# A decoder layer on one core: the first two blocks of the mixer's output projection computed as a pair, with three units of seven products

## The chip, the cores and the metric

The kernel runs on one core of a Trainium2 chip, as one program and one launch. The time is the device time of that core in microseconds (us). Its engines are named as in the profile: PE is TensorE (PEld its weight loads), DVE is VectorE, ACT is ScalarE, POOL is GpSimd, and SP is the engine whose queue issues most of the loads. Every engine works through its own queue of instructions in order and waits on semaphores for the others.

## The reference, cut to what matters

One layer on 256 tokens of width 2048 in float32: a mixer of two attention branches, whose outputs are gated, added and projected by `w_out`, and then a gated feed-forward part (FFN). Each of the two has a norm ahead of it and one behind it.

```python
merged = g[:, :, 0] * (o_a @ w_o_mla) + g[:, :, 1] * (o_b @ w_o_swa)
y = merged @ w_out                          # (256 x 2048) @ (2048 x 2048)
x = x + rms_norm(y, norm_mix_post)
x = x + rms_norm(conv_ffn(rms_norm(x, norm_ffn_pre)), norm_ffn_post)
```

## The kernel before

**Products.** The 256 tokens are two tiles of 128. Every float32 operand is split into a high and a low part, and one product of 128 tokens x 128 rows of the weight x 512 columns is three matmuls (`mm3`: high x high, high x low, low x high). `gemm` takes a block of 512 columns in eight chunks of two weight rows of tiles: a chunk of 128x1024 values is loaded into a `raw` tile by SP's queue (`wchunk`), ACT copies its high part (`whi`, L143), DVE subtracts to get the low part (`wlo`, L144), and PE does 12 matmuls with it, six for each token tile.

**The ring.** `raw` tiles come from a ring of 3, pairs of `whi` and `wlo` from a ring of 4 (`RING`). Two more tiles, `flex`, belong to the one or the other: while `flex[0]` is `"raw"` there are five raw tiles and four pairs, while it is `"w"` there are three raw tiles and five pairs. A pair comes free when the last matmul that reads it has run. `extra` gives some chunks a pair of their own from another pool; `px` holds three (`EXTRA`).

**Pairs of blocks.** `pair_gemm` computes two blocks of 512 columns at once, in units of two weight rows of tiles. A plain unit is eight products. A unit of seven (`seven`) forms sums of weight quarters on DVE and of the tokens' quarters ahead of time (`token_sums`), does seven products and leaves their recombination to a few DVE additions at the end; its raw rows are loaded by POOL's queue. Before the change it is used in a gate projection (`cg` in the profile) and in the FFN.

**The order of work.** Stages stand one after the other in the program. `at(t, f)` places small work into a later step (`tick`) of a running projection. What comes out is put in order by a scheduler, which also moves independent instructions among each other, on every engine.

**The stage in question.** The merge with `wo_a` (four blocks; `m_cols` transposes the merged values) is followed by `w_out` in four blocks, all by `gemm`, and by the FFN's first block. Ahead of `w_out`, `flex[0]` is set to `"w"`. In the last block, `split=0` runs the eight chunks for token tile 0 alone, and the products of tile 1 (`todo`, `finish_tile`) follow, with all eight pairs still held: five of the ring and three of `px`. `y_evac` squares a finished block on ACT and multiplies it by the norm's gain (`gpost`) on DVE. As soon as tile 0 of the last block is finished, `resid(0)` forms the inverse root (`rsqrt`, some ten DVE instructions on 128x1), adds to the residual stream `x2` (L987), transposes it on PE (`x2T`, L990), and splits it into the FFN's operand on ACT (L994) and DVE (L997). `resid(1)` does the same for tile 1.

Of the kernel before, what the change touches and what calls it, by code (L numbers as in the profile page):

```python
# [23 lines left out]
KT = D // P  # L24
# [17 lines left out]
def trunk_layer(ctx, tc, x, x_cols_in, conv_cols_in, g_mix_post, g_ffn_post, w_in, w_q, w_kv,  # L42
                sinks, rel, wo_a, wo_b, w_out, w_up, w_down, rope_tab, strip_sel, out):
    nc = tc.nc
    vec, act, pe, pool = nc.vector, nc.scalar, nc.tensor, nc.gpsimd

    def open_pool(name, bufs=1, **kw):
        es = ExitStack()
        return es, es.enter_context(tc.tile_pool(name=name, bufs=bufs, **kw))
# [3 lines left out]
    pss = ctx.enter_context(tc.tile_pool(name="pss", bufs=2, space=PS))  # L53
# [5 lines left out]
    def sb(pl, shape, name, dt=F32, tag=None, bufs=None):  # L59
        return pl.tile(shape, dt, name=name, tag=tag or name, **({"bufs": bufs} if bufs else {}))  # L60
# [43 lines left out]
    flex = ["raw"]  # L104
    turn = dict(raw=0, w=0)
# [10 lines left out]
    def wchunk(src, shape, own=None, rawp=None, rbufs=1, parts=None):  # L116
        i = cnt[0]
        cnt[0] += 1
        n = int(np.prod(shape))
        raw = rawp.tile([P, 1024], F32, name=f"raw{i}", tag="xraw", bufs=rbufs) if rawp else \  # L120
            ring_tile("raw", f"raw{i}", F32, in_turn("raw"))
        dst = raw[:, :n]
        if len(shape) == 2:
            dst = dst.rearrange("p (a b) -> p a b", a=shape[0])
        elif len(shape) == 3:
            dst = dst.rearrange("p (a b c) -> p a b c", a=shape[0], b=shape[1])
        if len(shape) == 3:
# [27 lines left out]
    now = [0]  # L155

    def at(t, *fs):
        steps[max(t, now[0])].extend(fs)
# [6 lines left out]
    def drain():  # L165
        while steps:
            tick()

    def new_acc(tag, ps=None):
        i = cnt[0]  # L170
        pl, pt = ps or (pacc, "acc")
        return [pl.tile([P, 512], F32, name=f"acc{tag}_{i}_{t}", tag=pt) for t in range(NT)]

    def mm3(o, ah, al, bh, bl, start, stop):
        pe.matmul(o, ah, bh, start=start, stop=False)  # L175
        pe.matmul(o, ah, bl, start=False, stop=False)  # L176
        pe.matmul(o, al, bh, start=False, stop=stop)  # L177
# [486 lines left out]
    acc, _ = gemm(XH, XL, w_in, 0, KT, 0, 512)  # L664
# [4 lines left out]
    acc, _ = gemm(XH, XL, w_in, 0, KT, C_KV, KVR + ROPE)  # L669
# [78 lines left out]
    AH, AL = pair_view(ath), pair_view(atl)  # L748
# [138 lines left out]
    b = now[0] + 26  # L887
# [11 lines left out]
    for j in range(4):  # L899
        acc, _ = gemm(XH, XL, w_in, 0, KT, C_GA + 512 * j, 512)  # L900
# [10 lines left out]
    mt = [slot("a", p) for p in range(8)]  # L911
    mth, mtl = highs(mt), lows(mt)
    MH_, ML_ = pair_view(mth), pair_view(mtl)
    x2_all = [sb(p3, [P, D], f"x2_{t}") for t in range(NT)]
    x2 = [[x_[:, j * 512:(j + 1) * 512] for j in range(4)] for x_ in x2_all]
    es6, p6 = open_pool("p6")
    gpost = sb(p6, [P, D], "gpost", tag="gp")

    def late_loads(i):

        if i < 4:
            nc.sync.dma_start(gpost[:, i * 512:(i + 1) * 512], g_mix_post[i * 512:(i + 1) * 512].partition_broadcast(P))
        else:
            t, j = divmod(i - 4, 4)
            nc.sync.dma_start(x2[t][j], x[t * P:(t + 1) * P, j * 512:(j + 1) * 512])

    esx, px = open_pool("px", bufs=EXTRA)
    es4, p4 = open_pool("p4")

    def m_cols(p, ld):  # L930
        pt = pst.tile([P, 512], F32, name=f"mT{p}", tag="t")
        for i in range(2):
            for t in range(NT):
                c = (2 * (p % 2) + i) * P
                pe.transpose(pt[:, i * 256 + t * P:i * 256 + (t + 1) * P], ld[t][0][:, c:c + P], ident)
        split_to(mth[p][:, :], mtl[p][:, :], pt, 0.5)
# [8 lines left out]
            ld.append((a, b))  # L945
        return ld

    for i in range(12):
        at(now[0] + 10 + 2 * i, lambda i=i: late_loads(i))
    for j in range(4):  # L950
        ld = merge_loads(j)
        acc, _ = gemm(AH, AL, wo_a, 0, KT, 512 * j, 512)
        for t in range(NT):
            a, b = ld[t]
            vec.scalar_tensor_tensor(a, a, 1.0, acc[t], op0=ALU.add, op1=ALU.mult)
            vec.tensor_tensor(a, a, b, op=ALU.add)
        for p in range(2):
            at(now[0] + (3 if j == 3 else 1) + p, lambda p=2 * j + p, ld=ld: m_cols(p, ld))


    yg_all = [[sb(p6, [P, 1024], f"yg_{t}_{j}", tag="f" + "ab"[t], bufs=2) for j in range(2)] for t in range(NT)]
    yg = [[yg_all[t][j // 2][:, (j % 2) * 512:(j % 2 + 1) * 512] for j in range(4)] for t in range(NT)]
    blocks = [(0, 512), (512, 512), (1024, 512), (1536, 256), (1792, 256)]
    NB = len(blocks)
    W_BLOCKS = [(512 * j, 512) for j in range(4)]
    ssy = [sb(p3, [P, 4], f"ssy{t}") for t in range(NT)]
    jk = lambda name: sb(p6, [P, 512], name, tag="jk", bufs=1)

    def y_evac(acc, b, t):
        c0, n = W_BLOCKS[b]  # L970
        j, o = c0 // 512, c0 % 512
        act.activation(jk(f"yj{b}_{t}")[:, :n], acc[t][:, :n], AF.Square, accum_out=ssy[t][:, b:b + 1])
        vec.tensor_tensor(yg[t][j][:, o:o + n], acc[t][:, :n], gpost[:, c0:c0 + n], op=ALU.mult)

    x2hl = [slot("b", p) for p in range(8)]
    HH, HL = pair_view(highs(x2hl)), pair_view(lows(x2hl))
# [31 lines left out]
        vec.tensor_scalar(r2, r, 0.5, None, op0=ALU.mult)  # L1008
        rf[t] = (r, r2)

    flex[0] = "w"
    turn.update(raw=0, w=0)
    for b in range(4):
        c0, n = W_BLOCKS[b]
        last = b == 3
        acc, todo = gemm(MH_, ML_, w_out, 0, KT, c0, n, split=0 if last else None, extra={i: (px,) for i in range(EXTRA)} if last else None)
        if b == 0:
            drain()
            es4.close()
            es8, p8 = open_pool("p8")  # L1020
        if last:
# [264 lines left out]
    def pair_end(i):  # L1286
# [46 lines left out]
EXTRA = 3  # L1333
# [69 lines left out]
```

## Time and profile before

| what | us |
|---|---|
| time, median of 3 runs | 1468.56 (1468.35 to 1468.61) |
| the profiled execution's own time | 1470.05 |
| its span, first to last instruction | 1468.3 |
| PE busy in the span | 1456.9 |
| DVE busy | 1067.2 |
| ACT busy | 830.5 |
| POOL busy | 64.9 |

The profile is of one execution. A row of its timeline gives the start, the length, the engine, the line of the kernel, and the tiles written and read, in brackets the idle time ahead and what ended it. A window's row gives the busy time of each engine (with instructions in brackets), the granted clock of TensorE and the load of the DMA queues. Matmuls overlap: one of 512 columns shows some 0.39 us, though the next starts earlier. The wait view names two waits of PE for another engine, both in the first 5 us.

### The profile page before, as it was taken

How to read it: one execution, taken by the hardware profiler on the slowest of the kernel's cores; microseconds unless marked ns; L12 is line 12 of the kernel's file. 1: busy time of each engine (PE TensorE's matmuls, PEld its weight loads, DVE VectorE, ACT ScalarE, POOL GpSimd, SP SyncE). 2: the span in 40 equal slices, each digit the busy share in tenths (PEclk: the TensorE clock that was granted, in tenths of full speed). 3: DMA queues.
4: the chain of work that ended last, by engine and by line, in shares of the span. 5: the costliest groups of instructions: out<-in, count | busy, mean ns of one | idle time of the engine just before them, and what ended most of it. 6: DMA issues, size and time to landing. Idle time of an engine off the chain costs nothing.

```text
span 1468.3 us, 20938 instructions
## 1 busy us (share of the span) xinstructions
PE 1456.9 (99%) x7576; PEld 1244.8 (85%) x7576; DVE 1067.2 (73%) x1881; ACT 830.5 (57%) x1372; POOL 64.9 (4%) x113
## 2 busy tenths in 40 slices
PE   9999999999999999999999999999999999999997
PEld 7888888888888888888888888888888888888886
DVE  7688896745667665555699976778776687677775
ACT  7588874543555554444566655555454565555453
POOL 0011110000000000000000000000000000000000
PEclk9999999999999999999999999999999999999999
DMA  8755376466655559756766666665656666667573
GB/s 297 211 164 167 108 259 192 162 212 200 191 156 160 164 163 334 226 184 212 225 205 185 188 193 193 187 187 187 218 174 213 198 187 189 187 197 233 163 237 129
DMA packets 149909, 287.60 MB, mean 196 GB/s; under 512 B 18428, under 2 KB 29597, under 8 KB 149677
## 3 DMA queue, kind: packets, MB, share of 16 engines
q1 hardware_dynamic: 141312, 256.80, 56.5%
q0 software_dynamic: 8400, 29.41, 6.4%
q8 instruction: 59, 0.97, 0.3%
q14 instruction: 46, 0.37, 0.1%
q10 hardware_dynamic: 92, 0.05, 0.0%
HBM read 277.79 MB, written 8.44 MB: 195 GB/s over the span
## 4 chain that ended last, share of the span: by engine, by line
PE 97%; DVE 2%; ACT 1%; issue 0%; DMA 0%; DVEq 0%; ACTq 0%
PE accg L175 13%; PE accg L177 13%; PE accg L176 13%; PE ub L1147 10%; PE ua L1147 10%; PE ua L1151 5%; PE ub L1151 5%; PE cd L177 2%; PE cd L175 2%; PE cd L176 2%; PE cdb L175 1%; PE cdb L177 1%; PE cdb L176 1%; PE mpo L875 1%; PE cg L176 1%; PE cg L177 1%
## 5 line engine op out<-in xcount | busy, mean ns | idle before, releaser
L144 DVE TENSOR_TENSOR wlo<-raw,whi 128x1024 fp32r<-128x1024 f32 (+2 forms) x476 | 576.3, 1214 | 282.5 <-ACT whi L143 275.2
L143 ACT CAST whi<-raw 128x1024 fp32r<-128x1024 f32 (+2 forms) x476 | 494.7, 1043 | 427.5 <-PE accg L177 172.3
L175 PE MATMUL accg<-whi,ahl 128*128 128x512 f32 (+1 forms) x480 | 187.9, 392 | 0.0
L177 PE MATMUL accg<-whi,ahl 128*128 128x512 f32 (+1 forms) x480 | 185.6, 387 | 0.0
L176 PE MATMUL accg<-wlo,ahl 128*128 128x512 f32 (+1 forms) x480 | 184.8, 385 | 0.0
L1147 PE MATMUL ua<-ahl,whi 128*128 128x512 f32 x640 | 154.6, 391 | 0.0
L1147 PE MATMUL ub<-ahl,whi 128*128 128x512 f32 x640 | 154.6, 391 | 0.0
L175 PE MATMUL accg<-whi,bhl 128*128 128x512 f32 x378 | 148.2, 392 | 0.0
L177 PE MATMUL accg<-whi,bhl 128*128 128x512 f32 x378 | 147.4, 390 | 0.0
L176 PE MATMUL accg<-wlo,bhl 128*128 128x512 f32 x378 | 147.3, 390 | 0.0
L1147 PEld LDWEIGHTS ub<-ahl,whi 128*128 128x128 f32 x640 | 117.5, 188 | 22.9 <-ACT cc L1045 0.2
L1147 PEld LDWEIGHTS ua<-ahl,whi 128*128 128x128 f32 x640 | 117.6, 188 | 22.7
L177 PEld LDWEIGHTS accg<-whi,ahl 128*128 128x128 f32 x480 | 90.1, 188 | 18.0
L176 PEld LDWEIGHTS accg<-wlo,ahl 128*128 128x128 f32 x480 | 90.3, 188 | 15.6
L175 PEld LDWEIGHTS accg<-whi,ahl 128*128 128x128 f32 x480 | 90.3, 188 | 15.5
L1151 PEld LDWEIGHTS ub<-ahl,wlo 128*128 128x128 f32 x640 | 82.2, 191 | 3.2
L1151 PEld LDWEIGHTS ua<-ahl,wlo 128*128 128x128 f32 x640 | 82.2, 191 | 3.1
L1151 PE MATMUL ua<-ahl,wlo 128*128 128x256 f32 x640 | 83.7, 283 | 0.0
L177 PEld LDWEIGHTS accg<-whi,bhl 128*128 128x128 f32 x378 | 71.0, 188 | 14.8
L176 PEld LDWEIGHTS accg<-wlo,bhl 128*128 128x128 f32 x378 | 71.0, 188 | 14.5
L1151 PE MATMUL ub<-ahl,wlo 128*128 128x256 f32 x640 | 83.2, 283 | 0.0
L175 PEld LDWEIGHTS accg<-whi,bhl 128*128 128x128 f32 x378 | 71.0, 188 | 14.3
(545 smaller groups left out, 2218.9 us busy)
## 6 DMA issues: line engine op xcount, KB each, us to landing
raw<-in_ffn_w_up_dram SPq DMA_DIRECT2D x176, 512.0 KB, 4.5
raw<-in_w_in_dram SPq DMA_DIRECT2D x105, 512.0 KB, 4.5
raw<-in_ffn_w_down_dram SPq DMA_DIRECT2D x68, 512.0 KB, 4.5
raw<-in_w_o_swa_dram SPq DMA_DIRECT2D x32, 512.0 KB, 4.4
raw<-in_w_o_mla_dram SPq DMA_DIRECT2D x32, 512.0 KB, 4.5
raw<-in_w_out_dram SPq DMA_DIRECT2D x32, 512.0 KB, 4.1
bias<-strip POOLq DMA_DIRECT2D x16, 256.0 KB, 4.4
raw<-in_mla_w_q_up_dram SPq DMA_DIRECT2D x32, 128.0 KB, 2.8
```

The lines of the kernel that those rows point to most:

```text
L143: act.copy(hi[:, a:b], raw[:, a:b])
L144: vec.tensor_tensor(lo[:, a:b], raw[:, a:b], hi[:, a:b].bitcast(F32), op=ALU.subtract)
L175: pe.matmul(o, ah, bh, start=start, stop=False)
L176: pe.matmul(o, ah, bl, start=False, stop=False)
L177: pe.matmul(o, al, bh, start=False, stop=stop)
L875: pe.matmul(o, w(t), p_[:, c], start=n == 0, stop=n == 5)
L1147: pe.matmul(acc[i], hi[:, c], hn[p][:, j * 512:(j + 1) * 512], start=p + j == 0, stop=stop)
L1151: pe.matmul(acc[i][:, 0:256], lo[:, c], hn[p][:, j * 512:j * 512 + 256], start=False, stop=False)
```

## The change

Blocks 0 and 1 of `w_out` become one `pair_gemm` of eight units in the order `ppspspsp` (p plain, s seven). The sums of the tokens' quarters for its three sevens (`m_sums`) are formed during the last two blocks of `wo_a`, in tiles of `px`. The raw rows of the first and third seven lie in `px` too, those of the second in the tile that `gpost` takes afterwards; so `gpost` is loaded later, by POOL's queue. The sums of the weight quarters take the place of `yg_all[t][1]`. `pair_evac` adds the recombined part, squares it and multiplies by the gain. Blocks 2 and 3 stay with `gemm`. The accumulators of the last `wo_a` block and of block 2 move to other PSUM banks. `flex[0] = "w"` now stands behind the `w_out` loop.

```diff
-    gpost = sb(p6, [P, D], "gpost", tag="gp")
+    gpost = []
...
-            nc.sync.dma_start(gpost[:, i * 512:(i + 1) * 512], g_mix_post[i * 512:(i + 1) * 512].partition_broadcast(P))
+            if i == 0:
+                gpost.append(sb(p6, [P, D], "gpost", tag="gp"))
+            pool.dma_start(gpost[0][:, i * 512:(i + 1) * 512], g_mix_post[i * 512:(i + 1) * 512].partition_broadcast(P))
...
+    def m_sums(u):
+        st = sb(px, [P, 1024], f"ms{u}", F32R, tag="w" + ("hi", "lo")[u % 2])
+        ms[u] = token_sums(mt[u].bitcast(F32), yg[0][0], yg[0][1], st[:, 0:512], st[:, 512:1024])
...
+        if j == 2:
+            for u in range(W_ORDER.count("s")):
+                at(now[0] + 2 + 4 * u, lambda u=u: m_sums(u))
+        acc, _ = gemm(AH, AL, wo_a, 0, KT, 512 * j, 512, ps=(pss, "s") if j == 3 else None)
...
-    flex[0] = "w"
-    turn.update(raw=0, w=0)
-    for b in range(4):
+    def w_place():
+        w_done[0] += 1
+        i = w_done[0]
+        if i % 2:
+            return [sb(px, [P, 1024], f"mr{i}{n}", tag="w" + n) for n in ("hi", "lo")]
+        both = sb(p6, [P, D], f"mr{i}", tag="gp")
+        at(now[0] + 2, *(lambda k=k: late_loads(k) for k in range(4)))
+        return both[:, 0:1024], both[:, 1024:2048]
+
+    def w_pair():
+        d = [yg[t][j] for t in range(NT) for j in range(2)]
+        c = pair_gemm("w", w_out, 0, 0, W_ORDER, lambda k, t: (MH_(k)[:, t * P:(t + 1) * P], ML_(k)[:, t * P:(t + 1) * P]),
+                      lambda u: ms[u], 0, d, w_place, lambda: [yg_all[t][1] for t in range(NT)])
+
+        def pair_evac(i):
+            t, j = divmod(i, 2)
+            vec.tensor_tensor(d[i], d[i], c[i], op=ALU.add)
+            act.activation(jk(f"yj{j}_{t}"), d[i], AF.Square, accum_out=ssy[t][:, j:j + 1])
+            vec.tensor_tensor(d[i], d[i], gpost[0][:, j * 512:(j + 1) * 512], op=ALU.mult)
+
+        for i in range(4):
+            at(now[0] + i, lambda i=i: pair_evac(i))
+
+    w_pair()
...
+    for b in range(2, 4):
...
+    flex[0] = "w"
+    turn.update(raw=0, w=0)
     first_extra = {0: (p8,)} | {i + 1: (px,) for i in range(EXTRA)}
...
+W_ORDER = "ppspspsp"
```

How the built order moves, at three places of the last `w_out` block and its end. First the queue of ACT. The casts `whi` of the last block's chunks carry the numbers 7041 to 7125 before and 7104 to 7188 after, as their `raw` tiles; `ffn` chunks begin with 7341 and 7404; `yj_0` squares token tile 0 of the finished last block. Before:

```order
L143 CAST whi_7103<-raw_7101 128x1024
L143 CAST whi_7115<-raw_7113 128x1024
L972 ACTIVATE yj_0_7033,ssy_6552<-accg_0_6887 128x512
L143 CAST whi_7127<-raw_7125 128x1024
L972 ACTIVATE yj_1_7036,ssy_6553<-accg_1_6888 128x512
L143 CAST whi_7343<-raw_7341 128x1024
L972 ACTIVATE yj_0_7137,ssy_6552<-accg_0_7039 128x512
```

And now:

```order
L143 CAST whi_7178<-raw_7176 128x1024
L143 CAST whi_7406<-raw_7404 128x1024
L143 CAST whi_7418<-raw_7416 128x1024
L143 CAST whi_7430<-raw_7428 128x1024
L143 CAST whi_7190<-raw_7188 128x1024
L143 CAST whi_7442<-raw_7440 128x1024
L143 CAST whi_7454<-raw_7452 128x1024
L983 ACTIVATE yj_0_7200,ssy_6571<-accg_0_7102 128x512
```

The eighth chunk's cast (`whi_7127`, now `whi_7190`) stood three rows ahead of the first square of the last block's sums and ahead of all FFN chunks; now three FFN chunks stand ahead of it. With the ring at four pairs it takes the place of the fourth chunk's pair, `whi_7142`, and its semaphore is set by the last matmul that token tile 1 does with that chunk.

Second, the queue of DVE from the start of tile 0's inverse root (`vy`, `ry_y`, `ry_t`, `ry_u` with 7140 before, 7203 now; 7324 is that of tile 1) to the first addition to the residual stream (`x_0`). Before:

```order
L984 TENSOR_SCALAR vy_7140<-vy_7140 128x1
L296 TENSOR_SCALAR ry_y<-vy_7140 128x1
L299 SCALAR_TENSOR_TENSOR ry_t<-vy_7140,ry_y 128x1
L306 TENSOR_SCALAR ry_t<-ry_t 128x1
L307 TENSOR_TENSOR ry_y<-ry_y,ry_t 128x1
L299 SCALAR_TENSOR_TENSOR ry_t<-vy_7140,ry_y 128x1
L144 TENSOR_TENSOR wlo_7356<-raw_7353,whi_7355 128x1024
L309 TENSOR_SCALAR ry_u<-ry_t 128x1
L310 TENSOR_TENSOR ry_u<-ry_u,ry_t 128x1
L144 TENSOR_TENSOR wlo_7368<-raw_7365,whi_7367 128x1024
L311 SCALAR_TENSOR_TENSOR ry_y<-ry_u,ry_y 128x1
L987 SCALAR_TENSOR_TENSOR x_0_5851<-yg_0_6548,ry_y,x_0_5851 128x512 x2
```

And now the first twelve rows of the same stretch:

```order
L995 TENSOR_SCALAR vy_7203<-vy_7203 128x1
L144 TENSOR_TENSOR wlo_7467<-raw_7464,whi_7466 128x1024
L296 TENSOR_SCALAR ry_y<-vy_7203 128x1
L144 TENSOR_TENSOR wlo_7479<-raw_7476,whi_7478 128x1024
L299 SCALAR_TENSOR_TENSOR ry_t<-vy_7203,ry_y 128x1
L994 TENSOR_REDUCE vy_7324<-ssy_6572 128x1
L984 TENSOR_TENSOR yg_1_5865<-accg_1_7103,gpost 128x512
L306 TENSOR_SCALAR ry_t<-ry_t 128x1
L995 TENSOR_SCALAR vy_7324<-vy_7324 128x1
L144 TENSOR_TENSOR wlo_7491<-raw_7488,whi_7490 128x1024
L307 TENSOR_TENSOR ry_y<-ry_y,ry_t 128x1
L296 TENSOR_SCALAR ry_y<-vy_7324 128x1
```

Between these and the first addition follow `wlo_7629`, the rest of tile 0's root and half of tile 1's. So four conversions of weights, tile 1's product with the gain and seven small instructions of tile 1's root stand in the stretch, where two conversions stood.

Third, PE around the first transposes of the residual stream (`x2T`); `accg_1_7040` and `accg_1_7103` are token tile 1 of the last `w_out` block, `accg_0_7402` is the FFN's first block. Before:

```order
L176 MATMUL accg_1_7040<-wlo_7092,ahl_5847 128x512
L177 MATMUL accg_1_7040<-whi_7091,ahl_5847 128x512
L990 MATMUL x2T_0_7155<-ident,x_0_5851 128x128 x4
L990 MATMUL x2T_1_7169<-ident,x_0_5851 128x128 x4
L175 MATMUL accg_1_7040<-whi_7091,ahl_5847 128x512
```

And now:

```order
L176 MATMUL accg_1_7103<-wlo_7191,ahl_5850 128x512
L177 MATMUL accg_1_7103<-whi_7190,ahl_5850 128x512
L1001 MATMUL x2T_0_7218<-ident,x_0_5851 128x128 x4
L1001 MATMUL x2T_1_7232<-ident,x_0_5851 128x128 x4
L175 MATMUL accg_0_7402<-whi_7406,bhl_6573 128x512
```

Before, 27 matmuls of tile 1 stood between tile 0's last one and these transposes, and 21 behind them. Now 14 stand between, and none of tile 1 is left behind: the next matmul needs the transposed values. Of tile 0's own six matmuls with the eighth chunk, the first stands behind 30 of tile 1's and the others behind 34; before, all six stood ahead of them. PE's queue has nine rows fewer in all.

More of the change, by code (lines that the diff above doesn't have):

```diff
@@ L946, in merge_loads @@
         return ld
-    for i in range(12):
+    yg_all = [[sb(p6, [P, 1024], f"yg_{t}_{j}", tag="f" + "ab"[t], bufs=2) for j in range(2)] for t in range(NT)]
+    yg = [[yg_all[t][j // 2][:, (j % 2) * 512:(j % 2 + 1) * 512] for j in range(4)] for t in range(NT)]
+    ms = {}
+    def m_sums(u):
+        st = sb(px, [P, 1024], f"ms{u}", F32R, tag="w" + ("hi", "lo")[u % 2])
+        ms[u] = token_sums(mt[u].bitcast(F32), yg[0][0], yg[0][1], st[:, 0:512], st[:, 512:1024])
+    for i in range(4, 12):
         at(now[0] + 10 + 2 * i, lambda i=i: late_loads(i))
@@ L951, in trunk_layer @@
         ld = merge_loads(j)
-        acc, _ = gemm(AH, AL, wo_a, 0, KT, 512 * j, 512)
+        if j == 2:
+            for u in range(W_ORDER.count("s")):
+                at(now[0] + 2 + 4 * u, lambda u=u: m_sums(u))
+        acc, _ = gemm(AH, AL, wo_a, 0, KT, 512 * j, 512, ps=(pss, "s") if j == 3 else None)
         for t in range(NT):
@@ L957, in trunk_layer @@
         for p in range(2):
-            at(now[0] + (3 if j == 3 else 1) + p, lambda p=2 * j + p, ld=ld: m_cols(p, ld))
-    yg_all = [[sb(p6, [P, 1024], f"yg_{t}_{j}", tag="f" + "ab"[t], bufs=2) for j in range(2)] for t in range(NT)]
-    yg = [[yg_all[t][j // 2][:, (j % 2) * 512:(j % 2 + 1) * 512] for j in range(4)] for t in range(NT)]
+            at(now[0] + (2 if j == 3 else 1) + p, lambda p=2 * j + p, ld=ld: m_cols(p, ld))
     blocks = [(0, 512), (512, 512), (1024, 512), (1536, 256), (1792, 256)]
@@ L972, in y_evac @@
         act.activation(jk(f"yj{b}_{t}")[:, :n], acc[t][:, :n], AF.Square, accum_out=ssy[t][:, b:b + 1])
-        vec.tensor_tensor(yg[t][j][:, o:o + n], acc[t][:, :n], gpost[:, c0:c0 + n], op=ALU.mult)
+        vec.tensor_tensor(yg[t][j][:, o:o + n], acc[t][:, :n], gpost[0][:, c0:c0 + n], op=ALU.mult)
     x2hl = [slot("b", p) for p in range(8)]
@@ L1009, in x2_norm @@
         rf[t] = (r, r2)
-    flex[0] = "w"
-    turn.update(raw=0, w=0)
-    for b in range(4):
+    w_done = [0]
+    def w_place():
[18 more added lines that the diff above has]
+    w_pair()
+    es4.close()
+    es8, p8 = open_pool("p8")
+    for b in range(2, 4):
         c0, n = W_BLOCKS[b]
         last = b == 3
-        acc, todo = gemm(MH_, ML_, w_out, 0, KT, c0, n, split=0 if last else None, extra={i: (px,) for i in range(EXTRA)} if last else None)
-        if b == 0:
+        acc, todo = gemm(MH_, ML_, w_out, 0, KT, c0, n, split=0 if last else None, extra={i: (px,) for i in range(EXTRA)} if last else None,
+                         ps=None if last else (pss, "s"))
+        if last:
             drain()
-            es4.close()
-            es8, p8 = open_pool("p8")
-        if last:
             y_evac(acc, b, 0)
```

## The prediction

> **What bounds the kernel now.** I read the page first, then the windows by stage, then the list of PE's waits.
>
> ```profile
> PE 1456.9 (99%) x7576; PEld 1244.8 (85%) x7576; DVE 1067.2 (73%) x1881; ACT 830.5 (57%) x1372; POOL 64.9 (4%) x113
> PE 97%; DVE 2%; ACT 1%; issue 0%; DMA 0%; DVEq 0%; ACTq 0%
> 645.00:735.00 90.00, 89.82 (x408) 74.01 (x407) 55.14 (x69) 45.85 (x69) 2.18 (x4) 1.00 0.67 216
> 735.00:785.00 50.00, 50.00 (x238) 41.74 (x237) 46.27 (x101) 32.58 (x62) 3.25 (x6) 1.00 0.64 200
> PE pstrip L349 <- DMA sel<-in_strip_sel_dram: 1.1, 1, 1.1
> PE warm L77 <- DVE ramp L66: 1.1, 1, 1.1
> ```
>
> PE carries 97% of the chain that ended last, and its only listed waits lie at the start. `w_out` runs from about 645 to 733.7, the FFN follows: in the first window PE is idle for 0.18 us in all, in the second for none. So in this stage the end is set by the number of matmuls alone. A matmul taken away gains its pitch; a stall put in is lost in full, since there is no idle time of PE downstream that could take it back. In the second window DVE is busy for 46 of 50 us: that is the point where another engine is nearest to the bound.
>
> **What the pair saves.** The pitch is read from the starts:
>
> ```profile
> 721.80 0.39 PE L175 MATMUL accg<-whi,ahl 128*128 128x512 f32 x1
> ...
> 726.34 0.39 PE L177 MATMUL accg<-whi,ahl 128*128 128x512 f32 x1
> ```
>
> These are 20 steps, (726.34 - 721.80) / 20 = 0.227 us. A plain unit has 8 products of 3 matmuls, a seven 7, so three sevens save 9 matmuls: 9 x 0.227 = **2.0 us** gained. That is 0.14% of the time, the most the arithmetic can give.
>
> Can DVE and ACT feed it? The gate projection runs the same arrangement, five plain units and three sevens, 183 matmuls:
>
> ```profile
> 242.70:284.50 41.80, 41.80 (x184) 34.12 (x183) 29.11 (x32) 21.91 (x23) 2.17 (x4) 1.00 0.44 148
> L144 DVE TENSOR_TENSOR wlo<-gta,whi 128x1024 fp32r<-128x1024 f32 x3 | 3.7, 1225 | 7.0 <-ACT whi L143 7.0
> L235 DVE TENSOR_TENSOR gtb<-gr,gtb 128x512 f32<-128x512 f32 x2 | 1.4, 689 | 0.0
> L143 ACT CAST whi<-gta 128x1024 fp32r<-128x1024 f32 x3 | 3.1, 1049 | 6.3 <-PE cg L177 6.3
> 252.01 4.62 DVE L144 TENSOR_TENSOR wlo<-raw,whi 128x1024 fp32r<-128x1024 f32 x4
> ```
>
> PE is never idle there, and 183 x 0.227 = 41.5 is the whole window. One seven costs DVE three conversions of 1024 at 4.62 / 4 = 1.16, one of 512 and four sums at about 0.6 each: 6.5 us against 21 x 0.227 = 4.8 on PE. A plain unit costs DVE 2.3 against 5.4. A seven with the plain unit behind it is thus 8.8 on DVE against 10.2 on PE, and ACT has less. The new order `ppspspsp` is closer packed at its end than the gate's, but it starts with two plain units, in which DVE runs ahead, and the token sums are formed earlier, under `wo_a`. The tightest place is the plain chunk behind the first seven, by this count: from the pair's start PE takes 11.8 us to the first seven (48 matmuls and two groups of transposes) and 16.5 to its end; that chunk's pair of the ring comes free 6 matmuls into the seven, at 13.4; DVE is then through the seven's other work at 15.1, and this conversion ends at 16.2, 0.5 us before the matmul that reads its low part. The cost is 0; bounds: 0 (as in the gate) and 2 us (that lead of 0.5 us lost for each seven, and once more when the block behind waits for the seven's banks). The four `gpost` loads, moved to POOL's queue, wait for the second seven's raw rows and stand behind the third seven's loads, so that they delay none of these; their reader comes two units later. Nothing on SP is delayed by leaving them out. With five raw tiles loads come earlier, which gains nothing, as PE waits for no load.
>
> **What the ring costs.** The second part of the change is the later `flex[0] = "w"`. The last `w_out` block holds all eight pairs until tile 1 has used them. Before, there were five in the ring and three of `px`; now the ring has four, so the eighth chunk waits for the fourth's pair. The built order shows what becomes of it: tile 0 can finish only when 34 of tile 1's 48 matmuls are done, and just 14 are left to cover what follows tile 0. What follows it, before:
>
> ```profile
> 720.22 0.39 PE L177 MATMUL accg<-whi,ahl 128*128 128x512 f32 x1
> ...
> 726.82 1.33 PE L990 MATMUL x2T<-ident,x 128*128 128x128 f32 x8
> ```
> ```profile
> 720.70 0.60 ACT L972 ACTIVATE yj<-accg 128x512 f32<-128x512 f32 x1 [2.31 <-PE accg L177]
> ```
> ```profile
> 721.42 0.16 DVE L983 TENSOR_REDUCE vy<-ssy 128x1 f32<-128x4 f32 x1 [1.77 <-ACT yj L972]
> 721.50 0.68 DVE L973 TENSOR_TENSOR yg<-accg,gpost 128x512 f32<-128x512 f32 x1
> 722.09 0.15 DVE L984 TENSOR_SCALAR vy<-vy 128x1 f32<-128x1 f32 x1
> 722.28 0.15 DVE L296 TENSOR_SCALAR ry_y<-vy 128x1 int32<-128x1 int32 x1
> ...
> 723.24 1.22 DVE L144 TENSOR_TENSOR wlo<-raw,whi 128x1024 fp32r<-128x1024 f32 x1
> ...
> 724.63 1.23 DVE L144 TENSOR_TENSOR wlo<-raw,whi 128x1024 fp32r<-128x1024 f32 x1
> 725.78 0.15 DVE L311 SCALAR_TENSOR_TENSOR ry_y<-ry_u,ry_y 128x1 f32<-128x1 f32 x1
> 725.97 2.74 DVE L987 SCALAR_TENSOR_TENSOR x<-yg,ry_y,x 128x512 f32<-128x512 f32 x4
> ```
>
> The reader sees the whole chain: tile 0's last matmul starts at 720.22, ACT squares, DVE forms the root in small dependent steps with two conversions pushed in between, the residual is added, and the first transpose starts at 726.82: 6.6 us. Under it lay 27 matmuls of tile 1, 27 x 0.227 = 6.1, and PE lost a quarter of a microsecond. I take four terms.
>
> (a) *Up to the first transpose.* DVE's queue now has in this chain two more conversions (2 x 1.16), one more product of 512 (0.6) and seven more small steps (about 0.1 each, as they fill each other's gaps): 6.6 + 3.6 = 10.2 us. Of this, 14 matmuls and the last one's own pitch cover 15 x 0.227 = 3.4. PE stands for **6.8 us**. Bounds: 3.2, if all the added rows fell into gaps of DVE (6.6 - 3.4), and 8.4, if ACT's casts, which stand in its queue between the two squares, hold DVE up by another 1.6.
>
> (b) *From there to the FFN's tile 1.* Before, 21 matmuls of tile 1 lay behind the first transposes. Now the FFN's first products come at once, and need the split result:
>
> ```profile
> 727.48 2.17 ACT L994 ACTIVATE bhl<-x2T,gmat 128x128 fp32r<-128x128 f32 x8 [1.70 <-PE x2T L990]
> 736.35 0.62 ACT L1002 ACTIVATE xj<-x 128x512 f32<-128x512 f32 x1
> 736.88 0.19 ACT L1002 ACTIVATION_READ_ACCUMULATOR xj<-x 128x1 f32 x1
> 729.76 2.15 DVE L997 SCALAR_TENSOR_TENSOR bhl<-x2T,gmat,bhl 128x128 fp32r<-128x128 f32 x8
> ```
>
> DVE has four more residual additions (2.74 / 4 = 0.68) in front of the first low part (0.3): 3.0 us after the transpose starts. PE fills 1.6 of these with two groups of transposes (0.44 each, with the change to and fro) and three matmuls, so it idles 1.4; behind that transposes, ACT's casts (0.27, with two squares of 0.8 ahead) and PE run nearly level, for which I add 0.2: **1.6 us**. Bounds: 0 and 4.
>
> (c) *The clock.* PE idle for long is clocked down:
>
> ```profile
> 1459.37 0.28 PE L177 MATMUL zb<-whi,ghl 128*128 128x256 f32 x1
> 1460.00:1464.00 4.00, 0.00 (x0) 0.00 (x0) 3.75 (x13) 0.80 (x3) 0.00 (x0) 0.78 0.17 62
> 6.43 2.67 PE acckv L415 x6
> 9.09 2.56 PE accq L415 x6
> 11.65 1.43 PE acckv L415 x6
> ```
>
> The last matmul ends at 1459.65; a mean clock of 0.78 over 1460 to 1464 means half speed from 1462.2 on, 2.6 us later. At the start of the kernel matmuls of 512 took 2.67 / 6 = 0.44 us until 11.65 and 1.43 / 6 = 0.24 afterwards. A stall of 6.8 us should therefore halve the clock for about 5 us behind it. Of the some 12 matmuls that this slows by 0.21 each (2.6 us), half lie under waits of (b): **1.2 us**. Bounds: 0 and 2.6. The Trainium skill, "TensorE: Matmul & The Clock Gate", Part 1, says that one idle window of about 3.4 us halves the clock and about 3.4 us of steady work restores it. The tail of this trace agrees that idling halves it, somewhat earlier. By the page (c) would be an estimated 0.8 us, and the sum 0.4 lower.
>
> (d) *The waiting cast itself.* From the fourth chunk's release ACT needs 1.05 and DVE 1.2 us for the eighth chunk; six matmuls of tile 1 lie ahead of the first that reads it, four more ahead of the next: 10 x 0.227 = 2.3, so 0. Behind that cast on ACT stand two FFN casts, which nobody waits for yet, and tile 0's square, which waits for PE longer than for them.
>
> Sum: -2.0 + 6.8 + 1.6 + 1.2 = +7.6. The profiled execution's span of 1468.3 becomes 1475.9; its own time of 1470.05 lies above the three runs, whose median, 1468.56, is 0.26 over the span. I forecast **1476.1 us**, 0.5% slower.
>
> **Rivals.** *The cover suffices.* If tile 1's remaining matmuls and the order of DVE hide the root, only the saving is left. It decides at a chain of 3.4 us from tile 0's last matmul to the first transpose; at 6.6, the chain of before, (a) is 3.2 and (b), (c) vanish. Times: 1466.5 to 1469.7, not slower by more than the measurement tells. For it: DVE idles 1.77 us ahead of its root in the row above, room for one conversion and a half. Against: its queue is in order, and the added rows stand behind the root's first step. The 0.01 is for a gain that I don't see. Chance 0.12, the 0.01 among it.
>
> *The sevens starve PE as well.* DVE falls behind in `spspsp`, each seven stalls, and block 2 waits for the banks of the recombination: 2 us on top of a boundary at its upper terms (8.4 + 2.6 + 2.6 - 2.0 + 2.0 = +13.6), about 1482; from 1480.5 on I count it here. For it: 6.5 on DVE against 4.8 on PE within a seven. Against: the gate's window. Chance 0.09.
>
> *The clock is not reduced*, the wait being broken by the transposes: 1474.9, within the forecast's own range.
>
> **How the numbers follow.** Forecast (a wait at the end of `w_out` of 5 to 14 us, net 1471.5 to 1480.5) 0.79, rivals 0.12 and 0.09. Range 1471.5 to 1480.5: below it is the covered case, above it the starved one. A difference of 0.2%, 2.9 us, is about what can be told from no change: the bounds are 1465.6 and 1471.5. Faster 0.01, same 0.11, slower 0.88.
>
> **What would show it.** PE's starts in the pair 0.227 apart with no gap, 183 matmuls; one idle stretch of 5 to 8 us ahead of the first `x2T`, its releaser DVE's residual addition; the eighth chunk's cast released by PE's matmul on `accg` of tile 1; granted clock below 1 in the next 5 us; from the FFN's second half on, everything as before, later by the sum. Wrong if `x2T` starts within 7 us of tile 0's last matmul, or if PE has gaps of more than 1 us among the sevens.

## The result, and the profile after

The changed kernel takes **1477.28 us** (median of 6 runs, 1475.37 to 1477.72) against 1468.51 of the kernel before on the same chip (1467.53 to 1468.81): a ratio of 1.0058, with a 95% interval of 1.0048 to 1.0067. The forecast was 1476.1 with a range of 1471.5 to 1480.5. The profiled execution took 1476.69 us, its span is 1474.9.

On the page of the changed kernel, the engines' busy time, then its list of PE's waits (us in total, times, longest):

```profile
PE 1456.6 (99%) x7567; PEld 1244.0 (84%) x7567; DVE 1089.1 (74%) x1925; ACT 838.5 (57%) x1382; POOL 70.2 (5%) x123
```
```profile
PE x2T L1001 <- DVE ry_u L309: 8.4, 1, 8.4
PE warm L77 <- DVE ramp L66: 1.1, 1, 1.1
PE pstrip L349 <- DMA sel<-in_strip_sel_dram: 0.4, 1, 0.4
```

PE does nine matmuls fewer than before (7567 for 7576) and has one wait that it did not have: 8.4 us ahead of the first transpose of the residual stream. The windows of the changed kernel, by stage: the pair, the last block, the wait, and what follows it (busy time of PE, PEld, DVE, ACT and POOL, granted clock, DMA share, GB/s):

```profile
642.00:684.60 42.60, 42.60 (x194) 35.23 (x193) 34.26 (x40) 22.85 (x25) 2.66 (x5) 1.00 0.49 158
706.00:728.00 22.00, 22.00 (x98) 17.88 (x97) 10.02 (x10) 9.58 (x14) 0.00 (x0) 1.00 0.46 140
728.00:737.00 9.00, 0.61 (x4) 0.19 (x3) 8.30 (x27) 4.18 (x7) 1.06 (x2) 0.64 0.76 238
737.00:742.00 5.00, 5.00 (x20) 4.02 (x21) 5.00 (x15) 4.91 (x17) 2.72 (x5) 0.62 0.98 342
```

In the pair PE is busy in all 42.60 us at full clock. Between 728 and 737 PE stands and DVE works (8.30 of 9), and the granted clock, 0.64 in the mean, falls to a half on the way. In the 5 us behind, PE counts as busy throughout, at a granted clock of 0.62 in the mean. PE's rows around the wait:

```profile
724.90 0.39 PE L177 MATMUL accg<-whi,ahl 128*128 128x512 f32 x1
...
728.10 0.39 PE L177 MATMUL accg<-whi,ahl 128*128 128x512 f32 x1
736.88 1.97 PE L1001 MATMUL x2T<-ident,x 128*128 128x128 f32 x8 [8.39 <-DVE ry_u L309]
...
739.29 0.63 PE L176 MATMUL accg<-wlo,bhl 128*128 128x512 f32 x1
739.72 0.63 PE L175 MATMUL accg<-whi,bhl 128*128 128x512 f32 x1
...
1466.82 0.28 PE L177 MATMUL zb<-whi,ghl 128*128 128x256 f32 x1
```

Tile 0's last matmul starts at 724.90; the 14 left over of tile 1 end the work at 728.10; the first transpose starts at 736.88. Behind it the matmuls start 0.43 apart, half speed. The last row is the last matmul of the program.

What ACT did ahead of the root. The first row is the eighth chunk's cast, which PE's matmul on `accg` released; the other two lie behind tile 0's last matmul:

```profile
721.50 1.05 ACT L143 CAST whi<-raw 128x1024 fp32r<-128x1024 f32 x1 [1.66 <-PE accg L177]
...
725.80 1.05 ACT L143 CAST whi<-raw 128x1024 fp32r<-128x1024 f32 x1 [1.12 <-PE accg L177]
726.75 0.59 ACT L983 ACTIVATE yj<-accg 128x512 f32<-128x512 f32 x1
```

And DVE from there to the residual addition:

```profile
726.88 1.23 DVE L144 TENSOR_TENSOR wlo<-raw,whi 128x1024 fp32r<-128x1024 f32 x1 [0.94 <-ACT whi L143]
728.02 0.15 DVE L994 TENSOR_REDUCE vy<-ssy 128x1 f32<-128x4 f32 x1
...
734.04 1.22 DVE L144 TENSOR_TENSOR wlo<-raw,whi 128x1024 fp32r<-128x1024 f32 x1 [0.70 <-ACT whi L143]
735.82 0.15 DVE L311 SCALAR_TENSOR_TENSOR ry_y<-ry_u,ry_y 128x1 f32<-128x1 f32 x1
736.08 0.74 DVE L998 SCALAR_TENSOR_TENSOR x<-yg,ry_y,x 128x512 f32<-128x512 f32 x1
```

The square was ready to run from about 725.3, but ACT had first to cast a chunk of the FFN, and that cast waited until 725.80 for a pair of the ring. DVE then converts the same chunk (726.88), and only behind it, at 728.02, comes the first step of the root. That is 3.12 us after tile 0's last matmul; before the change it was 721.42 - 720.22 = 1.20. Of the 1.9 us more, 1.4 are the square's later start (1.85 us behind that matmul, 0.48 before), and 0.5 the conversion that stands between the square and the root.

### The profile page after: what moved, and what is told of

Same layout as the page of the kernel before. It is cut to its first block, busy times and chain, and to the rows that moved or that the text cites. A ratio compares the mean times of both kernels' runs of the same rounds, so it can differ in the third digit from the quotient of the medians.

```text
span 1474.9 us, 20974 instructions
## 1 busy us (share of the span) xinstructions
PE 1456.6 (99%) x7567; PEld 1244.0 (84%) x7567; DVE 1089.1 (74%) x1925; ACT 838.5 (57%) x1382; POOL 70.2 (5%) x123
## 4 chain that ended last, share of the span: by engine, by line
PE 95%; DVE 3%; ACT 1%; DMA 0%; issue 0%; DVEq 0%; ACTq 0%
PE accg L175 12%; PE accg L177 12%; PE accg L176 12%; PE ub L1184 10%; PE ua L1184 9%; PE ub L1188 5%; PE ua L1188 5%; PE cd L177 2%; PE cd L175 2%; PE cd L176 2%; PE cdb L176 1%; PE cdb L175 1%; PE cdb L177 1%; DVE wlo L144 1%; PE mpo L875 1%; PE cg L175 1%
## 5 line engine op out<-in xcount | busy, mean ns | idle before, releaser
L144 DVE TENSOR_TENSOR wlo<-raw,whi 128x1024 fp32r<-128x1024 f32 (+2 forms) x470 | 568.6, 1215 | 254.1 <-ACT whi L143 246.3
L143 ACT CAST whi<-raw 128x1024 fp32r<-128x1024 f32 (+2 forms) x470 | 487.6, 1042 | 409.8 <-PE accg L177 161.8
L175 PE MATMUL accg<-whi,ahl 128*128 128x512 f32 (+1 forms) x416 | 162.4, 391 | 0.0
L177 PE MATMUL accg<-whi,ahl 128*128 128x512 f32 (+1 forms) x416 | 160.6, 386 | 0.0
L176 PE MATMUL accg<-wlo,ahl 128*128 128x512 f32 (+1 forms) x416 | 160.0, 385 | 0.0
L177 PEld LDWEIGHTS accg<-whi,ahl 128*128 128x128 f32 x416 | 78.1, 188 | 15.4
L176 PEld LDWEIGHTS accg<-wlo,ahl 128*128 128x128 f32 x416 | 78.2, 188 | 13.5 <-DVE wlo L144 0.3
L175 PEld LDWEIGHTS accg<-whi,ahl 128*128 128x128 f32 x416 | 78.1, 188 | 13.3 <-ACT whi L143 0.2
```

The lines of the kernel that those rows point to most:

```text
L143: act.copy(hi[:, a:b], raw[:, a:b])
L144: vec.tensor_tensor(lo[:, a:b], raw[:, a:b], hi[:, a:b].bitcast(F32), op=ALU.subtract)
```

## Experiments

The theory: the whole loss comes from the ring having four pairs in place of five in the last `w_out` block; the pair itself gains 2.0 us. The ratios are to runs of the kernel before on the same chip (1468.33, 1468.67 and 1468.46 us in the three groups of runs). A difference to the changed kernel's 1477.28 us, or from one group to another, is between groups, whose medians of before lie up to 0.3 us apart; beside such differences stands what the two traces show from the first transpose of the merged values (`mT`) to the program's last matmul: 878.81 us before, 887.45 in the changed kernel. All kernels do the same computation; e5 adds matmuls to it.

### e1: five pairs again in the last two blocks

```diff
     es8, p8 = open_pool("p8")
+    flex[0] = "w"
+    turn.update(raw=0, w=0)
     for b in range(2, 4):
...
-    flex[0] = "w"
-    turn.update(raw=0, w=0)
     first_extra = {0: (p8,)} | {i + 1: (px,) for i in range(EXTRA)}
```

> The changed kernel with the ring's switch to five pairs and three raw tiles put back ahead of the last two w_out blocks (behind the pair), nothing else. Theory (the ring's switch makes the whole loss): the eighth chunk gets a pair of its own again, tile 0 finishes with 27 of tile 1's matmuls left, PE's wait ahead of the first x2T falls from 8.4 us to under 0.5, the clock stays at 1.00 over the boundary, and the time is that of before less the nine matmuls: 1468.5 - 2.0 = 1466.5 us, about 10.8 under the changed kernel. Rival (the pair itself, by DVE's load or by its place, costs time): the wait falls but the time stays at or above 1468.5.

Measured: 1468.74 us (11 runs), ratio to before 1.0003 (0.9994 to 1.0011). PE's waits:

```profile
PE accg L176 <- DVE wlo L144: 1.4, 2, 0.8
PE warm L77 <- DVE ramp L66: 1.1, 1, 1.1
PE x2T L1001 <- DVE x L998: 0.4, 1, 0.4
```

The wait of 8.4 us is gone with two moved lines, and 8.5 us of the time with it; so the ring made the loss. But the pair's 2.0 us did not come through: two new waits of PE for low parts stand in the last block, 1.4 us. The time is where the rival had put it (1468.5 or more) and 2.2 us above the theory's 1466.5. Of the rival's two reasons, the pair's load on DVE does not show: PE has no wait in the pair here. What the casts waited for shows more. Groups of ACT's instructions, the casts between 690 and 718 us, first in this kernel, then in the kernel before (busy, mean ns, idle time ahead and what ended it):

```profile
L143 ACT CAST whi<-raw 128x1024 fp32r<-128x1024 f32 x12 | 12.6, 1050 | 14.1 <-DMA raw<-in_w_out_dram 12.5 <-DMA raw<-in_ffn_w_up_dram 1.6
```
```profile
L143 ACT CAST whi<-raw 128x1024 fp32r<-128x1024 f32 x12 | 12.6, 1053 | 14.9 <-DMA raw<-in_w_out_dram 7.9 <-PE accg L177 2.7 <-DMA raw<-in_ffn_w_up_dram 1.5
```

Before, part of the casts waited for PE to free a pair (2.7 us by this row): the ring was full, and chunks lay ready ahead of PE. Now all of them wait for loads: the ring is empty, and PE eats each chunk as it comes. The loads of this stretch on SP's queue, in one row of its timeline:

```profile
681.98 29.05 SPq L131 DMA_DIRECT2D raw<-in_w_out_dram  x12
```

With three raw tiles that is 2.4 to 2.6 us for each (29.05 / 12 or / 11). In the list of waits, from 690 to 718 us, this queue waits for DVE's subtractions:

```profile
SPq L131 <- DVE wlo L144: 22.1, 12, 2.3
```

So a load is issued when a conversion has freed a raw tile. From there the load takes 4.4 us to land (the median of the `w_out` loads in this window), the cast 1.05 and the subtraction 1.23: 6.7 us for one round of a tile, and with three tiles 2.2 for each chunk at best. A plain block takes 2.72 us per chunk (12 x 0.227), tile 0 alone in the last block 1.36. The new theory: each seven takes 0.68 us less (3 x 0.227), the loads do not follow, and the lead that carried the last block is missing. Whether the pair's own loads on POOL's queue have a part in it, no run separates.

### e2: the kernel before, with only the ring's switch moved

```diff
-    flex[0] = "w"
-    turn.update(raw=0, w=0)
     for b in range(4):
...
+    flex[0] = "w"
+    turn.update(raw=0, w=0)
     first_extra = {0: (p8,)} | {i + 1: (px,) for i in range(EXTRA)}
```

> The kernel before, without any pair, but with the ring's switch moved behind all of w_out, as in the change. Theory: the same wait appears without the pair, 8 to 9 us ahead of the first x2T and about 2 us behind it: +9 to +11 us against before, 1477.5 to 1479.5. Rival (the wait needs the pair's extra work on DVE and ACT): within 1 us of before, 1467.5 to 1469.5.

Measured: 1478.92 us (5 runs), ratio 1.0072 (1.0059 to 1.0084), +10.6 us.

```profile
PE x2T L990 <- issue: 8.6, 1, 8.6
```

The same wait without any pair (the view names no releaser here). The theory holds in size. The changed kernel, which has the pair as well, is 1.6 us faster than this one by the medians, though the intervals of the two ratios just overlap; from the first `mT` to the last matmul it is 889.41 us here and 887.45 there, 1.96 less. With the ring equal, the pair is worth its 2.0 us.

### e3: five pairs through all of `w_out`

The two lines stand ahead of `w_pair()`, as they stood ahead of `w_out` before the change.

> The changed kernel with the ring's switch put ahead of the pair, so that the whole of w_out has five pairs and three raw tiles, as before the change. Theory (the pair needs no five raw tiles): the same as with the switch behind the pair, 1466.5 us, within 0.4. Rival (the sevens need the two raw tiles, since a seven holds two of them at once): PE gets gaps among the sevens of 1 to 3 us together, 1467.5 to 1469.5.

Measured: 1467.69 us (11 runs, 1465.89 to 1469.79), ratio 0.9997 (0.9988 to 1.0006).

```profile
PE warm L77 <- DVE ramp L66: 1.1, 1, 1.1
PE accg L176 <- DVE wlo L144: 0.7, 1, 0.7
PE x2T L1001 <- DVE x L998: 0.5, 1, 0.5
```

The time is at the lower end of the rival's range, but the rival's mechanism is not there: no wait is among the sevens, they are in the last block, as in e1, and shorter. The pair needs no five raw tiles; the block behind it misses them (e8). Here the casts between 690 and 718 us wait 8.2 us for loads of `w_out`, and 4.0 are put down to DVE's subtractions, so this trace names the loads less plainly than e1's.

### e4: four pairs, and `px` serves the eighth chunk

```diff
-        acc, todo = gemm(MH_, ML_, w_out, 0, KT, c0, n, split=0 if last else None, extra={i: (px,) for i in range(EXTRA)} if last else None,
+        acc, todo = gemm(MH_, ML_, w_out, 0, KT, c0, n, split=1 if last else None, cont=True, extra={i: (px,) for i in (0, 1, 2, 7)} if last else None,
...
-            finish_tile(acc[1], todo)
+            finish_tile(acc[1], todo, cont=True)
```

`cont` lets tile 1 go on with the sum that the first chunk began.

> The changed kernel with the ring left at four pairs and five raw tiles, but the last block's first chunk is multiplied for both tiles at once, so that its px pair is free and serves the eighth chunk. Theory (the wait is for a hi/lo pair and for nothing else of the ring): 24 or more of tile 1's matmuls cover tile 0's evacuation again, the wait ahead of x2T is under 1.0 us, 1466.5 to 1467.5. Rival (it is the number or the order of the raw tiles, five in place of three, and the FFN casts that come early with them): the square still stands behind casts, the wait is 3 us or more, 1470 or more.

Measured: 1472.43 us (10 runs), ratio 1.0024 (1.0014 to 1.0033). PE's waits and, behind them, one row of ACT:

```profile
PE x2T L1001 <- DVE bhl L1008: 1.5, 1, 1.5
PE accg L176 <- DVE ry_u L309: 1.2, 1, 1.2
PE accg L175 <- ACT bhl L1005: 1.1, 1, 1.1
```
```profile
743.61 1.05 ACT L143 CAST whi<-raw 128x1024 fp32r<-128x1024 f32 x1 [3.53 <-DMA raw<-in_ffn_w_up_dram]
```

The mechanism is right and the time, which by itself would speak for the rival, is wrong. No wait is left ahead of the first transpose (these three come 11 us and more behind it), with five raw tiles as in the change: so the pairs made it and not the raw tiles. But the time came back in the FFN's first block: the three waits of 3.9 us together, and a stretch of half clock from 747.9 to 751.3 (last section). The ring switches there, and ACT's cast waited 3.53 us for a load; that the one made the other was not tested.

### e5: PE kept busy through the wait

```diff
             finish_tile(acc[1], todo)
+            idle = pss.tile([P, 512], F32, name="idle", tag="s")
+            for i in range(30):
+                tc.keep_in_program_order(pe.matmul(idle, mth[0][:, 0:P], mth[0], start=True, stop=True))
```

> The changed kernel with 30 more matmuls of 128x512, whose result nobody reads, between tile 1's last matmul and the first x2T: 30 x 0.227 = 6.8 us of PE work inside the wait of 8.4 us. Theory (the clock halves because PE idles): the granted clock stays at 1.00 behind the boundary, the first FFN matmuls start 0.23 apart instead of 0.43, and the time is 0.5 to 1.9 us under the changed kernel (1475.4 to 1476.8), the lower end only if PE and not DVE's low parts set the pace behind x2T. Rival (the half clock hides under waits for DVE): clock 1.00, but the time within 0.4 us of the changed kernel.

Measured: 1475.65 us (4 runs, 1475.18 to 1476.25), 1.6 under the changed kernel's median; ratio to before 1.0049 (1.0035 to 1.0063). Window and PE's rows:

```profile
737.00:742.00 5.00, 4.47 (x25) 3.26 (x23) 5.00 (x14) 4.94 (x18) 2.29 (x5) 1.00 1.03 367
```
```profile
736.07 1.38 PE L1001 MATMUL x2T<-ident,x 128*128 128x128 f32 x8 [1.58 <-DVE x L998]
...
1465.31 0.28 PE L177 MATMUL zb<-whi,ghl 128*128 128x256 f32 x1
```

The clock stays at 1.00. From the first transpose to the program's last matmul it is 729.24 us, in the changed kernel 1466.82 - 736.88 = 729.94: 0.7 us less by the profiles, 1.6 by the medians. The other 0.8 by which the two profiled spans differ lies ahead of the first `mT` (578.58 us here, 579.37 there), where the kernels are alike; and the intervals of the two ratios overlap. So the rival's bound of 0.4 is passed, by 0.7 in the stage itself; that the whole kernel is faster by more than this is not shown.

### e6 and e7: the last block begins with both tiles

The switch as in e3, with `split=1` (e6) and `split=2` (e7) and `cont=True` in the last block, and `px` for the first three chunks.

> The kernel with the ring's switch ahead of the pair, and in the last w_out block the first chunk is multiplied for both tiles at once, so that tile 0's own stretch asks for seven chunks in a row instead of eight. Theory (the pair's 2.0 us were given back because the last block's low parts come late: the sevens use the chunks up sooner, the loads with three raw tiles come one in 2.4 to 2.7 us as before, and tile 0 alone takes one in 1.36): the first chunk now takes 2.7 us, the late low parts (0.7 to 1.9 us of gaps) are caught up by 1.36, PE's waits in this block fall to 0.5 us or less, and the time is 1466.0 to 1467.2. Rival (the gaps come from the pair's work on DVE and ACT, which is done by then): the gaps stay and the time is within 0.4 us of the kernel with the switch ahead of the pair, 1467.3 to 1468.1.

> As the one before, with the first two chunks multiplied for both tiles at once. Theory: no late low part is left in the last block; but only 9 matmuls of tile 1, not 21, are left behind the first transposes, and the FFN's first products wait there for the split of x2T, up to 1.5 us: 1466.0 to 1468.5. Rival (the gaps are not a matter of loads): gaps of 0.7 us or more remain, 1467.5 or more.

Measured: e6 1470.05 us (11 runs), ratio 1.0011 (1.0002 to 1.0020); e7 1472.15 us (9 runs), ratio 1.0027 (1.0017 to 1.0036). Both missed. PE's waits in e6, then what ACT did there:

```profile
PE x2T L1001 <- DVE x L998: 3.0, 1, 3.0
```
```profile
719.88 1.05 ACT L143 CAST whi<-raw 128x1024 fp32r<-128x1024 f32 x1 [1.37 <-PE accg L177]
720.83 0.59 ACT L983 ACTIVATE yj<-accg 128x512 f32<-128x512 f32 x1
```

The late low parts are gone, as expected (the list has no wait on `accg`; in e3 it was 0.7 us). But the change of order put an FFN cast that waits for its pair ahead of tile 0's square: tile 0's last matmul starts at 718.07 here, the square at 720.83. This is the same queueing as in the changed kernel (725.80 and 726.75 above), in a kernel that has its eight pairs: the root's first step comes at 722.10, 4.0 us after tile 0's last matmul in place of 1.2, and the wait of 3.0 us is about that difference. In e7 the wait is 4.9 us: ahead of the square, which starts 4.55 us after tile 0's last matmul, stands an FFN cast that waited 1.40 us for its load.

### e8: the switch ahead of the last block alone

```diff
         last = b == 3
+        if last:
+            flex[0] = "w"
+            turn.update(raw=0, w=0)
...
-    flex[0] = "w"
-    turn.update(raw=0, w=0)
     first_extra = {0: (p8,)} | {i + 1: (px,) for i in range(EXTRA)}
```

> The changed kernel with the ring's switch put ahead of the last w_out block alone: five raw tiles and four pairs through the pair and the third block, three raw tiles and five pairs in the last. Theory (late loads): five raw tiles hold two more chunks loaded when the last block begins, the low parts are no longer late, gaps under 0.5 us, 1466.0 to 1467.2. Rival (at the switch the ring has to give two raw tiles up, which stops the loads at the worst moment): gaps of 2 us or more ahead of x2T, 1468.5 or more.

Measured: **1466.15 us** (11 runs, 1465.31 to 1466.83), ratio to before 0.9984 (0.9975 to 0.9993): faster than the change and than before. All of PE's waits, and ACT's casts between 690 and 718 us:

```profile
PE warm L77 <- DVE ramp L66: 1.1, 1, 1.1
PE pstrip L349 <- DMA sel<-in_strip_sel_dram: 0.2, 1, 0.2
```
```profile
L143 ACT CAST whi<-raw 128x1024 fp32r<-128x1024 f32 x12 | 12.4, 1052 | 12.8 <-DMA raw<-in_w_out_dram 5.7 <-PE accg L177 5.2 <-DMA raw<-in_ffn_w_up_dram 2.0
```

No wait is left but those of the start. The casts again wait for PE to free pairs (5.2 us, in e1 none): with five raw tiles up to the last block the loads are ahead once more, and with five pairs in it all eight chunks can be held. The gain of 2.5 us (by the interval 1.0 to 3.7) can hold the 2.0 of the nine matmuls: from the first `mT` to the last matmul it is 877.00 us, 1.8 less than before. Not all of the gain comes from there: behind the last matmul the two kernels without the pair (before and e2) take 8.93 and 8.77 us, the nine with it 8.06 to 8.14. Why, no run shows.

### e9: e8 with seven pairs

```diff
-        acc, todo = gemm(MH_, ML_, w_out, 0, KT, c0, n, split=0 if last else None, extra={i: (px,) for i in range(EXTRA)} if last else None,
+        acc, todo = gemm(MH_, ML_, w_out, 0, KT, c0, n, split=0 if last else None, extra={i: (px,) for i in range(2)} if last else None,
```

> The kernel with the ring's switch ahead of the last block (1466.15 us), but the last block's third chunk takes its pair from the ring and not from px: seven pairs for eight chunks, with three raw tiles and five pairs in the ring. Tile 0 then ends after 30 of tile 1's 48 matmuls, and 19 are left as cover, by the built order. Theory (the number of pairs alone makes the wait): a chain of 10 to 12 us from tile 0's last matmul to the first x2T, less 20 x 0.227 = 4.5, so a wait of 5.5 to 7.5 us and some 2 us behind it: 1473.5 to 1476. Rival (the number of raw tiles or the place of the switch makes it): within 1 us of 1466.15.

Measured: 1479.44 us (4 runs, 1477.01 to 1480.89), ratio 1.0078 (1.0061 to 1.0094).

```profile
PE x2T L1001 <- DVE x L998: 4.5, 1, 4.5
PE accg L175 <- ACT whi L143: 3.2, 1, 3.2
```

One pair taken away, and 13.3 us are lost against e8 by the medians, 11.75 by the traces (888.75 us from the first `mT` to the last matmul): the number of pairs does it, at an unchanged place of the switch. The size was missed, since the stop has two parts here: 3.2 us for the eighth chunk's own cast, which the theory left out, and 4.5 us ahead of the transpose, each with a stretch of half clock behind it (below).

## Why the prediction was right, point by point

**The pair: gain 2.0, cost 0.** Right in the changed kernel: PE never idles in the pair's window, and against e2 the pair gains 1.6 us by the medians, 1.96 by the traces. The place that was counted as tightest, the plain chunk behind the first seven, had a lead of 0.7 us where 0.5 were counted (the low part done at 657.12 + 2.35 / 2 = 658.3, read at 658.97). One sentence of this step fell: "With five raw tiles loads come earlier, which gains nothing, as PE waits for no load." As long as the ring's switch costs 8 us this can't be seen; with the switch put back (e1, e3) the low parts come late in the final block, in e1 plainly behind their loads, and most of the gain is gone: against before, e8 gains 2.5 us, e3 0.6, e1 nothing.

**The ring.** Right, and shown from both sides: moving the switch alone makes the loss (e2), moving it back takes it away (e1, e3, e8), freeing one pair with five raw tiles removes the wait (e4), taking one pair away with three raw tiles brings it back (e9).

**(a) Up to the first transpose, forecast 6.8, measured 8.4.** The cover was right (14 matmuls). From the root's first step to the transpose the forecast added 3.6 to 5.40; measured are 736.88 - 728.02 = 8.86, which is 3.5 more. So that step was right in sum. What was mis-sized lies ahead of the root: 3.12 in place of 1.20 us, 1.9 more. By the forecast's own count (the chain less 15 pitches) PE stands for 11.98 - 3.4 = 8.6 us; the view's 8.4 starts at the end of the last matmul, which is modelled. The prediction had it as its upper bound, "if ACT's casts, which stand in its queue between the two squares, hold DVE up by another 1.6", which gives 8.4, and did not take it; with the 0.5 of the conversion it is a little more. e6 shows the same cast ahead of the same square. The changed kernel with the square ahead of this cast was not tried, so that this part is read from the rows and from e6.

**(b) and (c), forecast 1.6 + 1.2, measured 2.2.** From the first transpose to the program's last matmul it was 1459.37 - 726.82 = 732.55 before, of which 21 matmuls of tile 1 are 4.77; now it is 729.94. 729.94 - (732.55 - 4.77) = 2.16. In e5, without the half clock, it is 1.46, so by the profiles (b) is 1.5 and (c) 0.7; by e5's median (c) would be 1.6. The forecast of 1.2 lies between the two; the traces, which compare this stage alone, speak for the smaller. The first low part came 3.0 us after the transposes' start (739.59 + 0.27 - 736.88), as forecast. But the 1.4 us for which PE was to idle there are not seen: in the change PE fills that time at half clock, and in e5 it idles for 0.5 of the 5 us (busy 4.47). So the size of (b) is right by the balance, and its parts are not shown. The half clock lasts 3.9 us behind the transposes' start, to 740.80, where about 5 were forecast.

**(d) The eighth chunk's own cast, forecast 0.** Two gaps of PE in the last block of 0.07 and 0.10 us, so 0.2. But this step ended with "tile 0's square, which waits for PE longer than for them" - for the FFN casts. That is the sentence that failed: one of these casts, released by PE's matmul at 725.80, ended after tile 0's last product, and the 1.9 us of (a) hang on it. It had been judged by the casts' length, and not by when their pair comes free. e9 shows that (d) itself is no constant either: there it is 3.2.

**Sum.** -2.0 + 8.4 + 2.2 + 0.2 = +8.8, against a forecast of +7.6; the traces give 887.45 - 878.81 = +8.6 from the first `mT` to the last matmul. The two spans differ by 6.6 only: up to the first `mT` this execution was 1.2 us shorter than that of before (579.37 and 580.56), and behind the last matmul 0.85 (8.08 and 8.93). So it is in part luck that the medians differ by 8.77, just as the sum does. Nor is the forecast as near as it looks: (a) was 1.6 to 1.8 us too small and (b) and (c) together 0.6 too large, which offset each other in part. The signs that the prediction named are there: the pair without gaps, one idle stretch behind tile 0 that ends with DVE (the view names `ry_u`; the residual addition that the transposes read ended at 736.82), the eighth chunk's cast released by PE (721.50), and a clock below 1 in the 5 us behind. The stretch is 8.4 us, over the 5 to 8 named.

**The rivals.** The cover did not suffice: the chain is 11.98 us, where 3.4 were needed. The sevens did not starve PE themselves; what they do to the loads behind them shows only when the ring is mended. The clock was reduced.

## What to carry to other kernels

A change that saves matmuls in a kernel bound by PE also takes time away from the loads and conversions beside it: look at what the casts wait for. Where part of them waited for a pair that PE frees (before, e8), the low parts came in time; where all waited for loads (e1), they came late. Resources that are shared by turns (here two tiles that are either raw or a pair) are worth a placing of their own for each block: where the same two lines stand decides over 11 us here (1477.28 in the change, 1466.15 in e8). And an instruction in an in-order queue waits for what those ahead of it wait for: when a small step on the critical chain is costed, ask of each row ahead of it when its buffer comes free, and not only how long it runs.

## What the runs showed of the hardware

The granted clock falls and rises in steps of one length. PE in e9 idles from 720.5 to 723.7 us and then works again; windows of 1 us:

```profile
722.00:723.00 1.00, 0.00 (x0) 0.00 (x0) 0.28 (x1) 1.00 (x2) 0.00 (x0) 1.00 0.48 49
724.00:725.00 1.00, 1.00 (x6) 0.75 (x4) 1.00 (x1) 0.00 (x0) 0.00 (x0) 0.98 0.46 174
725.00:726.00 1.00, 1.00 (x4) 0.77 (x3) 0.09 (x1) 0.75 (x1) 0.00 (x0) 0.50 0.72 131
728.00:729.00 1.00, 1.00 (x5) 0.82 (x4) 0.48 (x2) 1.00 (x3) 0.00 (x0) 0.81 1.00 268
735.00:736.00 1.00, 0.00 (x0) 0.00 (x0) 1.00 (x8) 0.00 (x0) 0.50 (x1) 0.60 0.72 121
742.00:743.00 1.00, 1.00 (x8) 0.87 (x7) 1.00 (x3) 0.82 (x3) 0.00 (x0) 0.99 1.05 424
```

The clock is full while PE stands (722 to 723) and is halved at 725.0, more than 1 us after PE resumed, until 728.4: 3.4 us. The second stretch lasts from 735.2 to 742.0, 6.8 us, twice that; in the changed kernel it is 730.56 to 740.80, 10.2, three times. It does not take one long wait. In e4 PE waited 1.14 us up to 744.97 and 1.53 us up to 747.00, and behind that the clock was halved from 747.9 to 751.3, 3.4 us again:

```profile
747.00:748.00 1.00, 0.99 (x6) 0.88 (x7) 1.00 (x5) 0.97 (x4) 0.00 (x0) 0.94 0.69 158
748.00:749.00 1.00, 1.00 (x4) 0.67 (x3) 0.17 (x3) 0.97 (x5) 0.00 (x0) 0.50 0.94 344
751.00:752.00 1.00, 1.00 (x5) 0.86 (x4) 0.95 (x5) 0.11 (x1) 0.00 (x0) 0.86 0.00 0
```

And a wait of 3.0 us (e6) halved nothing. So the length of a wait alone does not settle its price. Counted back by one length of 3.4 us from where the clock fell, PE had been idle for 2.0 us in e4, 2.1 in the changed kernel, 2.1 in e2 and 2.1 at e9's first fall (2.8 at its second, 3.4 in e7, whose wait of 4.9 us halved the clock too). That the idle share of such a stretch decides is a reading of these six, not tested; by it e6's wait would have to lie across two stretches, which no row shows. The Trainium skill, "TensorE: Matmul & The Clock Gate", Part 1, says that the clock is decided in free-running windows of about 3.4 us. The lengths here agree, and e4, where no wait was longer than 1.53 us, shows that a window need not be idle from end to end.
